# An encoder layer on one core: the MLP norm's scale moved into the first weights, its steps moved to ScalarE, a third tile for the mixers' output, query loads merged, and one combine of the differential attention moved to GpSimd

## The chip, the core and the metric

The kernel runs on one core of a Trainium2 chip. The metric is the time of one execution in device microseconds; for each kernel it is the median over several runs. TensorE is called PE in the profile (its weight loads PEld), VectorE DVE, ScalarE ACT, GpSimd POOL, and SyncE, which here only issues transfers, SP.

## The reference, cut to what matters

```python
n = rms_norm(h, g_mix);  z = n @ w_in                      # 1280 tokens (1024 + 256), width 1024
# mixer A: 4 heads, two softmax maps per head
sc = q @ k.T * scale - slope * |i - j|;  pr = softmax(sc)   # two maps, c = 0, 1
w  = pr[c=0] - lam * pr[c=1];  oa = rms_norm(w @ v, g_subln) * 0.8
# mixer B: 8 query heads on 2 key heads, rotary positions, plain softmax
h  = h + concat(oa, ob) @ w_out
n2 = rms_norm(h, g_mlp)                                     # n2 = h * rstd(h) * g_mlp
a  = relu(n2 @ w_ff1);  h = h + (a * a) @ w_ff2             # 1024 -> 4096 -> 1024
h  = h + sigmoid(rms_norm(h, g_ple) @ w_gate) * (p @ w_proj)
y  = rms_norm(h, g_final)
```

All is float32. `n2 @ w_ff1` is the same whether `g_mlp` (one number per input column) scales the columns of n2 or the rows of w_ff1.

## The kernel before, in words

A float32 product is made of three products of a shorter format: each operand is split into a high half (a rounded copy, usually by ACT) and a low half (the difference, by DVE or POOL), and high x high, high x low and low x high are summed in PSUM. So every matrix that TensorE reads costs ACT a copy and DVE or POOL a subtraction.

**Stages by time.** Input projections run to about 205 us, attention with the output projection woven in to about 730, the rest of the output projection, the MLP's norm and its transposes to about 824, the first MLP product to 1192, the second to 1586, gate and final norm to the end.

**Attention.** `plan_unit` (L509) plans units of 256 queries: for mixer A one unit per head and query block (two row blocks i = 0, 1 of 128 queries, two maps cc = 0, 1 each), for mixer B one per query head. Each step is put into a numbered round: scores (`qk`, L545) and, a round later, their row reduction on DVE (`mx`, L556; for A together with the distance term, L564, for B L568), the exponential on ACT (`ex`, L573 or L576), the combine (`cb`, L579), then transposes (L605), their halves on ACT (L611) and DVE (L616), and the product with the values (`av`, L629). A unit in the first 1024 tokens is "full": its rows are 1024 wide. In `cb` a mixer-A row block takes the reciprocals of both row sums (L583, DVE), scales the first map on POOL (L584), makes `-lam / sum` (L585, DVE) and adds the scaled second map to the first (L586, DVE). Row block 0 is combined two rounds before row block 1; the transposes read both. Steps after the attention product (L640 to L669) use POOL too (L660 to L663).

`load_q` (L471) fetches the 256 queries of a unit twice, into partitions 0 to 63 and 64 to 127, in four transfers of 128 KB: two copies by two maps.

**The weave.** The side work (`side_work`, L852: the remaining query and key projections, then two passes of the output projection) is a generator. The loop over rounds (L874) takes pieces from it in proportion to each round's cost; a piece of cost 0.0 ends the side work of that round. So `for _ in range(Y[k]): yield 0.0` lets a round go by without filler. What is left of the side work after the last round is done in the loop at L1066.

**Output projection** (`out_proj`, L801). The first pass takes four of the eight heads' outputs, the second the other four. For each of ten token tiles it loads the mixers' output `mt` (512 KB, L820) into W6 and W7 in turn, and makes two groups of twelve products (`pso`). Its weights come through `opw_dma` and `opw_split` (ACT L797, POOL L798). `Y = (2, 0, 0)` gives the empty turns: between the weight splits, before the remaining splits, and after the load of the first tile.

**MLP norm** (`mlp_norm`, L935). When a token tile is done in the second pass, its rows are stored (`hd`), squared and summed on ACT (L943), `rsqrt` (L130) makes the reciprocal root in six steps that change between DVE and ACT (L133, L134, L135, L137, L138, L139), and DVE multiplies the rows by it and by `g_mlp` in two halves of 512 columns (L948). `g_mlp` lies as a full tile in the last columns of two MLP operand tiles (`gbc`), filled by a broadcast from memory (L915 to L919). Then come transposes (L960), copies (`nb`, L968), sums and differences of 128 x 512 (L989) for a seven-product scheme (a 2 x 2 block product with seven instead of eight block products), and high and low halves (`n_split`, L1055, L1056; `nhi`, `nlo`).

**First MLP product.** `w_ff1` comes in 16 column blocks of 256. `w1_load` (L929) fetches one in two halves of 512 KB into W8, W9 and W10 in turn (`w1r`). `w1_ops` (L1010) makes the seven weight operands of a block: sums on POOL (L1026, L1027, L1032, L1036; on DVE for block 0), high halves on ACT (L1020), low halves on DVE or POOL (L1021). It runs one block ahead, one step after each product. The first block is started early: its loads are asked for at the start of the loop at L1066.

**What sets the order.** Within an engine's queue the order is fixed when the program is built. The builder places instructions by its own estimate of times, with the program's order as priority, so a queue's order is not always that of the lines: the first `w_ff1` load is issued at 467.44 us, in the middle of the attention, although its line stands after it. Tags such as W8 name a place in SBUF; a new tile in it waits until the former one has been read.

## Time and profile before

| | us |
|---|---|
| median of 3 runs | 1740.61 (1740.08 to 1741.46) |
| the profiled execution | 1741.92 |
| its span, first to last instruction | 1740.1 |

The page gives each engine's busy time and share of the span. Groups of instructions are named line, engine, operation, output<-inputs. A wait is written as "who <- whom: total us, times, longest". In a timeline row the first number is the start, the second the length, both in us, and the bracket says how long the engine stood idle before it and what ended that. In a row of busy time by stretch come the stretch, its length, the busy time of each engine with its instructions, TensorE's granted clock, the share of time the 16 transfer engines were busy, and GB/s.

### The profile page before, as it was taken

How to read it: one execution, taken by the hardware profiler on the slowest of the kernel's cores; microseconds unless marked ns; L12 is line 12 of the kernel's file. 1: busy time of each engine (PE TensorE's matmuls, PEld its weight loads, DVE VectorE, ACT ScalarE, POOL GpSimd, SP SyncE). 2: the span in 40 equal slices, each digit the busy share in tenths (PEclk: the TensorE clock that was granted, in tenths of full speed). 3: DMA queues.
4: the chain of work that ended last, by engine and by line, in shares of the span. 5: the costliest groups of instructions: out<-in, count | busy, mean ns of one | idle time of the engine just before them, and what ended most of it. 6: DMA issues, size and time to landing. Idle time of an engine off the chain costs nothing.

```text
span 1740.1 us, 27190 instructions
## 1 busy us (share of the span) xinstructions
PE 1675.2 (96%) x9868; PEld 1494.0 (86%) x9868; DVE 1182.7 (68%) x2115; ACT 852.7 (49%) x1715; POOL 598.3 (34%) x549
## 2 busy tenths in 40 slices
PE   8999988999989999998999999999999999999997
PEld 8999877888878887878999999998888888888886
DVE  7857468778778887579866666665664855354665
ACT  7522267767767666456333333333333333344554
POOL 1324445645654444431523332320433400001442
PEclk9999999999999999999999999999999999999999
DMA  9723653432873532282534333339665365532111
GB/s 306 229 80 109 194 163 104 121 122 86 235 207 105 157 103 79 92 271 87 182 130 152 128 131 141 142 137 385 232 227 194 120 209 191 179 112 83 39 44 49
DMA packets 188598, 263.45 MB, mean 151 GB/s; under 512 B 13104, under 2 KB 121520, under 8 KB 188464
## 3 DMA queue, kind: packets, MB, share of 16 engines
q1 hardware_dynamic: 186864, 256.47, 45.7%
q0 software_dynamic: 1600, 5.24, 1.0%
q8 instruction: 78, 1.28, 0.3%
q14 instruction: 56, 0.46, 0.1%
HBM read 175.16 MB, written 81.27 MB: 147 GB/s over the span
## 4 chain that ended last, share of the span: by engine, by line
PE 80%; DVE 7%; DMA 6%; ACT 3%; issue 2%; POOL 1%; SPq 1%; POOLq 0%; DVEq 0%; ACTq 0%
PE psg L151 6%; PE pso L220 5%; PE sc L551 5%; PE av L629 5%; PE psa L220 5%; PE tr L605 3%; PE psb L220 3%; PE psv L220 2%; PE psp L151 1%; DVE p L564 1%; DVE p L586 1%; DMA xr<-in_xT 1%; DMA mt<-md 1%; DMA xt<-in_x 1%; DVE pl L616 1%
## 5 line engine op out<-in xcount | busy, mean ns | idle before, releaser
L551 PE MATMUL sc<-kt,qt 128*128 128x512 f32 (+1 forms) x576 | 156.5, 395 | 18.2 <-DVE mm L564 7.2
L1231 ACT ACTIVATE ao<-ar 128x1280 fp32r<-128x1280 f32 x56 | 71.2, 1272 | 190.9 <-PE f__16190 L151 37.8
L1233 DVE TENSOR_TENSOR ao<-ar,ao 128x1280 fp32r<-128x1280 f32 x56 | 94.4, 1686 | 100.8 <-ACT ao L1231 100.8
L616 DVE TENSOR_TENSOR pl<-tr,ph 128x512 fp32r<-128x512 f32 x204 | 137.8, 683 | 33.7 <-ACT ph L611 32.9
L611 ACT ACTIVATE ph<-tr 128x512 fp32r<-128x512 f32 x204 | 120.2, 596 | 76.6 <-PE tr L605 63.1
L551 PEld LDWEIGHTS sc<-kt,qt 128*128 128x128 f32 x576 | 100.0, 190 | 39.1 <-DVE mm L564 11.3
L220 PE MATMUL pso<-ow,mt 128*128 128x512 f32 x480 | 122.7, 402 | 5.9 <-ACT ow L797 3.3
L605 PE MATMUL tr<-ident,p 128*128 128x128 f32 x768 | 117.0, 276 | 10.0 <-DVE pl L616 9.5
L151 PE MATMUL psg<-gw,n 128*128 128x512 f32 (+1 forms) x504 | 114.9, 384 | 0.0
L605 PEld LDWEIGHTS tr<-ident,p 128*128 128x128 f32 x768 | 92.1, 142 | 26.5 <-issue 8.5
L220 PEld LDWEIGHTS pso<-ow,mt 128*128 128x128 f32 x480 | 89.7, 193 | 24.2 <-ACT ow L797 3.8
L151 PEld LDWEIGHTS psg<-gw,n 128*128 128x128 f32 x504 | 90.9, 188 | 19.0
L629 PE MATMUL av<-ph,vt 128*128 128x256 f32 x544 | 103.5, 292 | 0.1
L1020 ACT ACTIVATE w<-w1s 128x512 fp32r<-128x512 f32 x64 | 40.1, 627 | 122.4 <-POOL w1s L1036 6.5
L568 DVE TENSOR_REDUCE mm<-sc 128x1 f32<-128x1024 f32 (+1 forms) x80 | 83.7, 1054 | 15.1 <-PE sc L551 14.5
L590 POOL TENSOR_SCALAR p<-p,rl 128x1024 f32<-128x1024 f32 x64 | 76.0, 1189 | 47.7 <-DVE rl L588 40.5
L629 PE MATMUL av<-pl,vt 128*128 128x256 f32 x408 | 91.7, 307 | 0.0
L629 PEld LDWEIGHTS av<-ph,vt 128*128 128x128 f32 x544 | 84.1, 194 | 4.9 <-DVE h_sb L840 0.3
L564 DVE CUSTOM_DVE_ANT_0 p<-sc,dist 128x1024 f32<-128x1024 f32 x64 | 77.1, 1217 | 13.4 <-PE sc L551 6.6
L576 ACT ACTIVATE p<-sc,mm 128x1024 f32<-128x1024 f32 x64 | 71.4, 1116 | 24.9 <-DVE mm L568 17.2
L573 ACT ACTIVATE p<-p,mm 128x1024 f32<-128x1024 f32 x64 | 73.4, 1148 | 12.7 <-DVE mm L564 11.6
L1406 POOL TENSOR_TENSOR p_l<-pr,p_h 128x256 fp32r<-128x256 f32 x10 | 7.8, 782 | 182.7 <-ACT p_h L1405 182.7
(1510 smaller groups left out, 4713.0 us busy)
## 6 DMA issues: line engine op xcount, KB each, us to landing
ar<-ad SPq DMA_DIRECT2D x56, 640.0 KB, 4.1
w2r<-in_w_ff SPq DMA_DIRECT2D x56, 512.0 KB, 4.5
qt<-qd SPq DMA_DIRECT2D x160, 128.0 KB, 3.2
ad<-q SPq DMA_DIRECT2D x64, 320.0 KB, 2.2
w1r<-in_w_ff SPq DMA_DIRECT2D x32, 512.0 KB, 3.8
ad<-qs SPq DMA_DIRECT2D x48, 320.0 KB, 2.2
md<-ml SPq DMA_DIRECT2D x40, 256.0 KB, 2.6
mt<-md SPq DMA_DIRECT2D x20, 512.0 KB, 4.6
```

The lines of the kernel that those rows point to most:

```text
L151: PE.matmul(ps, a, b, start=start and i == 0, stop=stop and i == n - 1)
L220: PE.matmul(ps, a, b, start=i == 0, stop=i == n - 1)
L551: PE.matmul(ps[:, h0:h0 + n], shared["q"][:, cc, v, i * P:(i + 1) * P], kt[:, s0 + h0:s0 + h0 + n], start=v == 0, stop=v == 1)
L564: V.tensor_tensor_reduce(out=p[:, :sn], in0=ps[:, :sn], in1=dst_t[:, off:off + sn], scale=SLOPES[idx], scalar=3.0e38, op0=ALU.add, op1=ALU ...
L568: V.tensor_reduce(out=st["m", i][:, 0:1], in_=ps[:, :sn], axis=AX.X, op=ALU.max, negate=True)
L573: S.activation(p[:, :sn], p[:, :sn], AF.Exp, scale=-1.0, bias=st["m", i][:, cc:cc + 1], accum_out=st["l", i][:, cc:cc + 1])
L590: G.tensor_scalar(p[:, :sn], p[:, :sn], rl[:, 0:1], 1.0, op0=ALU.mult, op1=ALU.mult)
L605: PE.transpose(t[:, jj, i * P:(i + 1) * P], st["ws"][i][:, j * P:(j + 1) * P], ident)
L611: S.activation(ph, st["tr", j2], AF.Copy)
L616: V.tensor_tensor(pl, st["tr", j2], f(st["ph", j2][:]), op=ALU.subtract)
L629: PE.matmul(st["av"][:, :256], x_, y_, start=j2 == 0 and n == 0, stop=j2 == nj - 1 and n == len(pr) - 1)
L1233: V.tensor_tensor(ao[:, 1], a, f(ao[:, 0]), op=ALU.subtract)
```

## The change

It does seven things.

1. `g_mlp` is loaded as a column tile (4 KB, after `gple`), the broadcast copy `gbc` and its loads are gone, and `w1_ops` first multiplies each of a block's eight weight slices (128 x 256) by its column of `g_mlp`, in place, on POOL.
2. `mlp_norm` runs on ACT alone: after the square, seven instructions on 128 x 1 (logarithm, mean plus eps, exponential, and one refinement step in four), then one copy of 128 x 1024 scaled by the result. DVE's two multiplications are gone.
3. `mt` gets W8 as a third place, in the whole first pass and in the first six tiles of the second; the last four tiles alternate between two.
4. As W8 is taken until then, the loads of the first block of `w_ff1` are asked for when six tiles of the second pass are done.
5. `Y = (2, 0, 2)`: two empty turns after the load of the first tile, in each pass.
6. `load_q` uses two transfers of 256 KB; the layout of `qt` is (operand half, map) in one index.
7. In `cb`, row block 0 of a full mixer-A unit scales the second map on POOL (by `-lam / sum`, in place) and adds the two maps on POOL. Row block 1 and the units of 256 tokens stay as they were.

```diff
-    Y = (2,0,0)
-    QM = 0
+    Y = (2,0,2)
...
+    gmlp = cp.tile([P, KD], F32, name="gmlp")
+    eps6 = cp.tile([P, 1], F32, name="eps6")
+    V.memset(eps6, 1e-6)
+    c15 = cp.tile([P, 1], F32, name="c15")
+    V.memset(c15, 1.5)
...
     gple = col("gple", g_ple, KD)
+    load(gmlp, g_mlp)
...
-        "qt": ([P, 2, 2, 256], F32R, QTB), "p": ([P, 1024], F32, PB), "dist": ([P, DISTW], F16, 1),
+        "qt": ([P, 4, 256], F32R, QTB), "p": ([P, 1024], F32, PB), "dist": ([P, DISTW], F16, 1),
...
         for dup in range(2):
-            for c in range(2):
-                dma(f(qt[dup * 64:(dup + 1) * 64, c]),
-                    qd[i][:, c * 64:(c + 1) * 64, t0:t0 + 256].rearrange("v d t -> d v t"))
+            dma(f(qt[dup * 64:(dup + 1) * 64]),
+                qd[i][:, :, t0:t0 + 256].rearrange("v (c d) t -> d (v c) t", d=64))
...
-                    PE.matmul(ps[:, h0:h0 + n], shared["q"][:, cc, v, i * P:(i + 1) * P],
+                    PE.matmul(ps[:, h0:h0 + n], shared["q"][:, 2 * v + cc, i * P:(i + 1) * P],
...
                 G.tensor_scalar(p[:, :sn], p[:, :sn], rl[:, 0:1], 1.0, op0=ALU.mult, op1=ALU.mult)
-                V.tensor_scalar(rl[:, 1:2], rl[:, 1:2], neglam, None, op0=ALU.mult)
-                V.scalar_tensor_tensor(p[:, :sn], p1[:, :sn], rl[:, 1:2], p[:, :sn], op0=ALU.mult, op1=ALU.add)
+                if i == 0 and full:
+                    G.tensor_scalar(p1, p1, rl[:, 1:2], neglam, op0=ALU.mult, op1=ALU.mult)
+                    G.tensor_tensor(p, p, p1, op=ALU.add)
+                else:
+                    V.tensor_scalar(rl[:, 1:2], rl[:, 1:2], neglam, None, op0=ALU.mult)
+                    V.scalar_tensor_tensor(p[:, :sn], p1[:, :sn], rl[:, 1:2], p[:, :sn], op0=ALU.mult, op1=ALU.add)
...
-            mt = slot(f"W{6 + next(mt_n) % 2}", [P, 4, 2, P], F32R, "mt")
+            mt = slot(("W6", "W7", "W8")[it % 3 if first or it < 6 else it % 2], [P, 4, 2, P], F32R, "mt")
...
-    gbc = [f(LO[i][:, :, HT - P:]) for i in (2, 3)]
-    gd = dp.tile([1, D], F32, name="gd")
-    dma(gd, g_mlp)
-    for i in range(2):
-        dma(gbc[i], gd[:, i * 512:i * 512 + 512].to_broadcast([P, 512]).rearrange("p (k t) -> p k t", t=P))
...
         S.activation(hn[t], h, AF.Square, accum_out=ss)
-        rs = ntp.tile([P, 1], F32, tag="nrs", name="nrs", bufs=2)
-        rsqrt(rs, ss, 1.0 / D, 1e-6, ntp, 1, f"n{half}")
-        for i in range(2):
-            c = slice(i * 512, i * 512 + 512)
-            V.scalar_tensor_tensor(hn[t][:, c].rearrange("p (k t) -> p k t", t=P),
-                                   h[:, c].rearrange("p (k t) -> p k t", t=P), rs, gbc[i], op0=ALU.mult, op1=ALU.mult)
+        u, v, rs = (ntp.tile([P, 1], F32, tag=f"n{n}{half}", name=f"n{n}", bufs=1) for n in "uvr")
+        S.activation(u, ss, AF.Ln, scale=1.0 / D, bias=eps6)
+        S.activation(v, ss, AF.Identity, scale=1.0 / D, bias=eps6)
+        S.activation(rs, u, AF.Exp, scale=-0.5)
+        S.activation(u, rs, AF.Square)
+        S.activation(u, u, AF.Copy, scale=v)
+        S.activation(u, u, AF.Identity, scale=-0.5, bias=c15)
+        S.activation(rs, rs, AF.Copy, scale=u)
+        S.activation(hn[t], h, AF.Copy, scale=rs)
...
         r0, r1 = w1raw.pop(p)
+        for k in range(KD):
+            r = (r0, r1)[k // 4][:, k % 4]
+            G.tensor_scalar(r, r, gmlp[:, k:k + 1], 1.0, op0=ALU.mult, op1=ALU.mult)
...
-        if n == 0:
+        if len(op_done) >= 6 and ops0 is None:
             w1_load(0, 0)
             w1_load(0, 1)
             ops0 = w1_ops(0)
```

More of the change, by code (lines that the diff above doesn't have):

```diff
@@ L473, in load_q @@
         for dup in range(2):
-            if QM:
-                dma(f(qt[dup * 64:(dup + 1) * 64]), qd[i][:, :, t0:t0 + 256].rearrange("v (c d) t -> d c v t", d=64))
-                continue
-            for c in range(2):
-                dma(f(qt[dup * 64:(dup + 1) * 64, c]),
-                    qd[i][:, c * 64:(c + 1) * 64, t0:t0 + 256].rearrange("v d t -> d v t"))
+            dma(f(qt[dup * 64:(dup + 1) * 64]),
+                qd[i][:, :, t0:t0 + 256].rearrange("v (c d) t -> d (v c) t", d=64))
         return qt
@@ L777, in encoder_kernel @@
     ow_n = itertools.count()
-    mt_n = itertools.count()
     def opw_dma(ch):
@@ L1056, in n_split @@
         lo_eng.tensor_tensor(LO[i][:, :, c], src, f(HI[i][:, :, c]), op=ALU.subtract)
-    trs, steps, normed = transposes(), 0, 0
+    trs, steps, normed, ops0 = transposes(), 0, 0, None
     w1raw = {}
@@ L1504 @@
         "w_gate": c(np.asarray(w_ple_gate)[0]), "w_proj": c(np.asarray(w_ple_proj)[0]),
-        "g_mix": c(np.asarray(g_mix)[0].reshape(KD, P).T), "g_mlp": c(np.asarray(g_mlp)[0].reshape(1, D)),
+        "g_mix": c(np.asarray(g_mix)[0].reshape(KD, P).T), "g_mlp": c(np.asarray(g_mlp)[0].reshape(KD, P).T),
         "g_ple": c(np.asarray(g_ple)[0].reshape(KD, P).T), "g_subln": c(np.asarray(g_subln)[0].reshape(P, 1)),
```

## The prediction

> **What bounds the kernel now.** I read the page's engine totals first, then busy time by stage, then the list of what TensorE waited for.
>
> ```profile
> PE 1675.2 (96%) x9868; PEld 1494.0 (86%) x9868; DVE 1182.7 (68%) x2115; ACT 852.7 (49%) x1715; POOL 598.3 (34%) x549
> ```
> ```profile
> 205.00:730.00 525.00, 488.76 (x3010) 425.15 (x3010) 404.93 (x741) 352.51 (x718) 262.68 (x275) 0.98 0.47 135
> 770.00:782.00 12.00, 11.49 (x60) 9.58 (x59) 11.31 (x22) 7.10 (x17) 4.40 (x6) 1.00 1.04 313
> 782.00:800.00 18.00, 17.25 (x97) 15.89 (x97) 17.58 (x30) 13.81 (x28) 2.29 (x4) 1.00 0.41 138
> 800.00:824.00 24.00, 18.96 (x127) 17.90 (x126) 23.65 (x39) 14.46 (x25) 3.53 (x3) 0.86 0.21 67
> 824.00:1192.00 368.00, 368.00 (x2505) 368.00 (x2504) 243.26 (x410) 130.60 (x258) 125.40 (x89) 1.00 0.43 153
> ```
> ```profile
> PE tr L605 <- DVE pl L616: 9.5, 13, 1.8
> PE sc L551 <- DVE mm L564: 7.2, 9, 2.0
> PE sc L551 <- ACT p L576: 6.0, 6, 1.7
> PE sc L551 <- DMA qt<-qd: 4.6, 1, 4.6
> PE pso L220 <- ACT ow L797: 3.3, 2, 3.1
> PE pso L220 <- DMA mt<-md: 2.6, 2, 2.1
> PE f__10380 L151 <- ACT nhi L1055: 2.1, 1, 2.1
> ```
>
> After the stretch come its length and the busy time of PE, PEld, DVE, ACT and POOL. TensorE is busy 96% of the span and never stops in the first MLP stage (368.00 of 368), so only its waits can be won, and nearly all of them lie in the attention (205 to 730 us) and in the passage to the MLP (730 to 824 us). In the attention they end mostly on DVE or on ACT work that DVE released. From 770 to 824 us DVE is the full engine: 52.5 of 54 us, beside ACT's 35.4.
>
> **The combine of the first map sum, attention.** One unit, in order of time:
>
> ```profile
> 637.89 1.12 POOL L584 TENSOR_SCALAR p<-p,rl 128x1024 f32<-128x1024 f32 x1 [6.17 <-PE sc L551]
> 639.05 1.28 DVE L586 SCALAR_TENSOR_TENSOR p<-p,rl 128x1024 f32<-128x1024 f32 x1 [0.38 <-POOL p L584]
> 640.25 1.22 DVE L564 CUSTOM_DVE_ANT_0 p<-sc,dist 128x1024 f32<-128x1024 f32 x1
> 641.53 1.19 PE L551 MATMUL sc<-kt,qt 128*128 128x512 f32 x4 [2.02 <-DVE mm L564]
> ```
> ```profile
> 239.60 0.44 PE L605 MATMUL tr<-ident,p 128*128 128x128 f32 x2 [1.17 <-DVE pl L616]
> 711.52 0.30 PE L605 MATMUL tr<-ident,p 128*128 128x128 f32 x1 [1.78 <-DVE pl L616]
> ```
> ```profile
> L586 DVE SCALAR_TENSOR_TENSOR p<-p,rl x32: 1264/1359/2235, 235.1 to 714.9; 128x1024 f32<-128x1024 f32 x32
> L1239 POOL TENSOR_TENSOR kt<-w2r,kt x8: 2392/2407/3320, 1295.5 to 1344.1; 128x1024 f32<-128x1024 f32 x8
> ```
> ```profile
> 297.49:304.15 6.66, 5.00 (x7) 1.00 0.67 192
> 422.86:429.77 6.91, 5.42 (x6) 1.00 0.48 141
> sum 149.76, POOL 74.63; mean POOL 4.66
> ```
>
> The first combine (row block i = 0) even makes DVE wait for POOL (0.38 us), and the next score reduction, for which TensorE waits, stands behind it. I followed every such wait back through DVE's unbroken busy run: 20 of them, the first at 239.60 and the last at 711.52 us, 17.9 us together, have a first combine in that run. They belong to 13 of the 16 full mixer-A units. Capped at what the edit takes out of the run (a combine of about 1.4 us and a 128x1 scale of about 0.2, like the small DVE step L138 quoted with the norm below), they are 15.9 us: the most that can be won.
>
> DVE loses 16 x (1.36 + 0.21) = 25 us of 404.93. POOL gets per unit a scale like L584 (1.12 us) and an add; the nearest row for that is L1239's median, 2.41 us. That is 3.53 us a unit, 56 us in all: POOL goes to 319 of 525 us. It must fit between a unit's two POOL scales, for the second combine stays on DVE behind the second scale. The 16 intervals last 149.76 us and POOL is busy for 74.63 of them, so 4.7 us are free on average; the two tightest, quoted, leave 1.66 and 1.49, one more 3.25. There the second scale comes 1.9, 2.0 and 0.3 us late, 4.2 us in all. The transposes need both row blocks, and the second is combined 7 to 14 us after the first, so the first one's longer POOL path holds nobody. Ends -15.9 (every wait goes) and +4.2 (none goes, every lateness is paid). I take -7, somewhat under half, because the exponentials and copies on ACT come next: at 711.52 TensorE waited for a low half that also needs ACT's high half.
>
> The Trainium skill, "SBUF — State Buffer", section "Who interferes with whom", says that a DVE instruction with two SBUF inputs and a GpSimd one that reads SBUF shut each other out for the whole instruction. The trace agrees: L586 takes 1264 ns alone and up to 2235. By that rule a 2.41 us add can hold a second combine for its whole length, at most 16 x 2.41 = 39 us of DVE time, where the rows of L586 give the -7 above.
>
> **Two more empty turns before the first output tile.**
>
> ```profile
> 700.00:720.00 20.00, 17.22 (x103) 14.65 (x103) 16.71 (x29) 13.85 (x29) 12.28 (x14) 0.91 0.04 14
> ```
>
> In the first pass this moves the first tile two rounds back, behind the weight split that TensorE awaited for 3.1 us (L797). The loop has some 220 rounds, 525/220 = 2.4 us each. In the quoted stretch they ran without filler and TensorE idled 14%, 0.33 us a round. So -3.1 + 0.7 = -2.4; ends -3.1 and +1.4 (the wait stays and the idle share doubles). The second pass has no such wait: +0.7, ends 0 and +1.4. The filler itself is only done later.
>
> **Third tile for the mixers' output, and the first MLP weights after it.**
>
> ```profile
> 745.14 7.79 DMA mt<-md
> 752.98 6.12 PE L220 MATMUL pso<-ow,mt 128*128 128x512 f32 x19 [2.12 <-DMA mt<-md]
> ```
>
> In the second pass the sixth tile was loaded when the fourth was done, took 7.79 us and cost 2.1. With three places it is asked for a tile earlier: -2.1. The last four tiles have two places again, so the other 0.5 us of this wait stays. The place is W8, so the first two w_ff1 loads (1 MB) now come when the sixth tile, begun at 752.98, is done, not long before the transfers are full (share 1.04 at 313 GB/s from 770 us): 3.4 us of transfer ahead of the eighth to tenth tiles. TensorE has transposes there; I take +0.7. Sum -1.4, ends -2.6 and +1.3 (all 3.4 against the 2.1). On SP these loads wait for W8; behind them stand tile loads whose place is free only two tiles later. In the first pass the third place frees SP from waiting, but no wait of TensorE there ends on mt: 0.
>
> **The norm on ACT.** The last tile's path now:
>
> ```profile
> 793.65 1.05 ACT L943 ACTIVATE hn<-h_sb 128x1024 f32<-128x1024 f32 x1
> 797.76 0.15 DVE L133 TENSOR_SCALAR n1v<-nss 128x1 f32<-128x1 f32 x1
> 798.42 0.19 ACT L134 ACTIVATE n1u<-n1v 128x1 f32<-128x1 f32 x1
> 800.95 0.21 DVE L138 SCALAR_TENSOR_TENSOR n1v<-nrs,n1v 128x1 f32<-128x1 f32 x1
> 802.96 1.41 DVE L948 SCALAR_TENSOR_TENSOR hn<-h_sb,nrs,nlo 128x512 f32<-128x512 f32 x2
> 803.85 1.79 PE L960 MATMUL trn<-ident,hn 128*128 128x128 f32 x8 [2.77 <-ACT nhi L1055]
> ```
>
> From the square's start to the transposes go 10.2 us, most of it in DVE's queue. As a row on ACT: 1.05 + 7 x 0.2 + 1.05 = 3.5 us. A tile takes 1.9 us off DVE (0.15, 0.21, one more such small step, 1.41) and puts 1.8 on ACT (four more small steps, one copy of 128x1024 like the square). With four tiles normalised from 770 to 824 us, DVE goes from 52.5 to 45, ACT from 35.4 to 43 of 54 us. But from 782 to 800 us ACT gets 13.81 + 2 x 1.8 = 17.4 of 18 and becomes the full engine. The waits to be had are 2.8 and 2.1, 4.9 us. I take -2, ends -4.9 and +2 (one tile's extra ACT work in front of the high halves).
>
> **The scale folded into w_ff1, on POOL.**
>
> ```profile
> L584 POOL TENSOR_SCALAR pq<-pq,rl x8: 477/482/1559, 293.4 to 674.2; 128x256 f32<-128x256 f32 x8
> 820.19 0.63 ACT L1020 ACTIVATE w<-w1r 128x512 fp32r<-128x512 f32 x1 [4.76 <-DMA w1r<-in_w_ff]
> 820.31 1.29 POOL L1026 TENSOR_TENSOR w1s<-w1r 128x512 f32<-128x512 f32 x1 [25.52 <-DMA w1r<-in_w_ff]
> 821.68 1.62 POOL L1027 TENSOR_TENSOR w1s<-w1r,w1s 128x512 f32<-128x512 f32 x1
> 823.91 1.55 PE L151 MATMUL f__10596<-nhi,w 128*128 128x384 f32 x8
> 781.30 1.22 PE L151 MATMUL f__10336<-nhi,w 128*128 128x384 f32 x6
> ```
>
> Eight scales of 128x256 at 0.48 us are 3.84 us a column block. The first block's, on weights that land some 10 us after the sixth tile, are done well before its first product, now at 781.30: 0, and 3.84 without that cover. From the third block on it is covered: each weight is split a whole unit, 7 x 3.5 = 24.5 us, before its product, and POOL goes to 125.40 + 15 x 3.84 = 183 of 368 us. Without that cover it would cost 58 us. The second block has little cover: landing at 820.2, scales to 824.0, the two differences to 826.9, split on ACT and DVE (0.63 + 0.69) to 828.2, while the second product is due at 823.91 + 3.5 = 827.4. So +0.8; ends 0 (the half that landed early is scaled first) and +3.8.
>
> **The rest.**
>
> ```profile
> 220.00:225.00 5.00, 0.75 (x2) 0.69 (x3) 0.90 (x2) 1.98 (x4) 1.95 (x2) 0.88 1.10 273
> ```
>
> Two query loads for four halve SP's issues, but the one wait for them (4.6 us) lies where the transfers are full (1.10) and the bytes are the same: 0, ends -4.6 (it goes) and +0.5 (TensorE now waits for a whole load, 128 KB more at 273 GB/s). The dropped broadcast of g_mlp and the added 4 KB load have no waiter: 0.
>
> **Sum** against the profiled execution, 1741.92 us (span 1740.1 and 1.8 around it): -7 - 2.4 + 0.7 - 1.4 - 2 + 0.8 = -11.3, so 1730.6. The median of the runs, 1740.61, lies 1.3 below the profiled one: 1729.3.
>
> **Rivals.**
> - *The attention's waits only move.* TensorE then waits for ACT, or for queues that the build's own ordering has laid out anew. For it: ACT is busy 67% there and releases the 6.0 us row. Against: in the unit at 637 us nothing but DVE stands between. Gain of the other terms alone: 1741.92 - 4.3 - 1.3 = 1736.3.
> - *POOL becomes the late engine, slower.* If the add takes 5 us, held off by DVE, the extra is 6.1 us a unit, and the 16 intervals are short by 27.6 us together. The second combine then heads DVE's queue and waits. With half of that on TensorE and the 7 us not won: 1730.6 + 7 + 13.8 - 1.3 = 1750. It decides once the add is over 3.6 us (4.7 free less 1.12). Against it: L1239's slowest is 3320 ns. The skill's SBUF page, by the rule above, is what would make it so.
> - *All waits behind the first combine and in the passage go.* -15.9 and -4.9 in place of -7 and -2: 1729.3 - 8.9 - 2.9 = 1717.5.
>
> **Chances.** Forecast 0.60 (its own range 1722 to 1738), waits move 0.20, POOL late 0.10, all go 0.10. A measurement of this kernel can tell about 0.2%, 3.5 us. The first rival lies near that bound, some of it inside; with the forecast's upper edge that makes faster 0.79, same 0.11, slower 0.10. The range, 1716 to 1743, leaves out the slower rival and the outermost of the rest.
>
> **What would show it.** Right: between 205 and 730 us DVE near 380 us and POOL near 320; the three DVE-bound rows of TensorE's waits down by about 7 us; the row on L797 gone; mt waits under 1.5; the last tile's square to transposes under 6 us; TensorE still 100% busy in the first MLP stage, with at most 2 us lost before its second block. Wrong: a POOL add over 3.6 us or DVE idle behind POOL at the second combine; ACT full from 782 to 800 us with high halves later; a new wait on mt after 765 us; an attention stretch of 525 us or more.

## The result, and the profile after

The changed kernel is slower: 1755.72 us (median of four runs, 1752.23 to 1757.44) against 1740.34 (median of four, 1739.75 to 1741.46). The ratio is 1.0085, 95% interval 1.0067 to 1.0103. The profiled execution of the changed kernel took 1752.23 us, with a span of 1750.5; it is the fastest of its four, so the two profiles show 10.3 of the 15.4 us between the medians.

The page first, with the engine totals, and then busy time by stage (stretch, length, PE, PEld, DVE, ACT, POOL, PE's granted clock, transfer share, GB/s):

```profile
PE 1682.0 (96%) x9868; PEld 1494.7 (85%) x9868; DVE 1158.5 (66%) x2035; ACT 870.4 (50%) x1765; POOL 717.9 (41%) x709
```
```profile
205.00:730.00 525.00, 484.89 (x2980) 416.62 (x2979) 381.22 (x707) 351.48 (x717) 310.78 (x307) 0.99 0.48 133
770.00:782.00 12.00, 12.00 (x62) 10.14 (x61) 7.50 (x13) 10.39 (x25) 5.97 (x9) 1.00 0.95 304
782.00:800.00 18.00, 17.60 (x96) 15.48 (x95) 15.50 (x20) 15.96 (x33) 3.74 (x5) 1.00 0.71 221
800.00:824.00 24.00, 14.53 (x77) 13.39 (x76) 19.21 (x27) 19.93 (x38) 8.53 (x9) 0.72 0.08 26
824.00:1192.00 368.00, 367.46 (x2498) 367.19 (x2497) 253.55 (x408) 127.82 (x256) 187.66 (x202) 1.00 0.42 143
```

The loads moved between engines as forecast: in the attention DVE went from 404.93 to 381.22 and POOL from 262.68 to 310.78. But TensorE was busy for less there (484.89 instead of 488.76), and from 800 to 824 us it fell from 18.96 to 14.53, at a granted clock of 0.72 instead of 0.86. What TensorE waited for:

```profile
PE sc L552 <- ACT p L577: 14.3, 11, 6.7
PE tr L610 <- DVE pl L621: 10.2, 16, 1.7
PE trn L962 <- ACT hn L951: 9.4, 2, 6.4
...
PE sc L552 <- DVE mm L565: 5.4, 7, 1.2
...
PE pso L224 <- ACT ow L801: 1.0, 1, 1.0
...
PE f__10577 L155 <- DVE w L1026: 0.5, 1, 0.5
```

The waits on `mt` (2.6 us before) and on the query loads `qt` (4.6) are gone, and that on `ow` is down from 3.3 to 1.0 us. The attention's waits on DVE have stayed: those on the reductions `mm` fell from 7.2 to 5.4, those on the low halves `pl` rose from 9.5 to 10.2. The waits on ACT's exponentials rose from 6.0 to 14.3, and there is a new row: the norm's transposes wait 9.4 us for ACT's copy `hn`.

Of the 14.3 us, 6.7 are one wait at the very start of the attention, and it goes with the query loads, not with the combine. TensorE waits there for an exponential, the exponential for row maxima on DVE, and these stand in DVE's queue behind a step on `zl`, which waited 7.49 us until a store (`kd<-zl`) had read its place:

```profile
220.18 0.69 DVE L742 SCALAR_TENSOR_TENSOR zl<-psa,R 128x512 f32<-128x512 f32 x1 [7.49 <-DMA kd<-zl]
222.03 1.11 ACT L577 ACTIVATE p<-sc,mm 128x1024 f32<-128x1024 f32 x1 [0.50 <-DVE mm L569]
223.29 3.78 PE L552 MATMUL sc<-kt,qt 128*128 128x512 f32 x8 [6.73 <-ACT p L577]
```

All thirteen kernels of this case that merge the query loads have this wait (5.3 to 6.8 us) and none on `qt`. The seven that do not have 3.3 to 4.6 us on `qt` at the same place.

**A table by stage** serves all that follows. Its marks are TensorE's own products in the trace: the first score product, the last product of the output projection, the end of the first column block of the first MLP product (its 168th product), the start of the third block, the ends of the first and second MLP product and of the gate. All in us, from the profiled executions:

| kernel | attention and output projection | passage (of it to the last transposes) | second block | blocks 3 to 16 | second product | gate | from the third block on |
|---|---|---|---|---|---|---|---|
| before | 575.4 | 35.2 (16.8) | 24.5 | 345.8 | 390.2 | 142.9 | 878.8 |
| after | 574.5 | 42.6 (26.4) | 25.4 | 347.7 | 390.5 | 143.4 | 881.6 |

What comes before the first score product took 213.4 and 214.5 us, what follows the gate 12.7 and 11.8. So the 10.3 us of the profiles are 7.4 in the passage, 0.9 in the second block, 2.8 after it, and -1.0 in the attention's column, where -10.1 was forecast.

The 7.4 us of the passage have two parts. Its rows, before and after:

```profile
788.90:824.10 35.20, 29.41 (x188) 28.00 (x188) 34.85 (x56) 21.72 (x39) 4.38 (x4) 0.90 0.21 68
```
```profile
789.00:831.60 42.60, 32.73 (x197) 30.59 (x197) 36.01 (x53) 33.44 (x66) 14.71 (x18) 0.84 0.25 78
```

TensorE stands idle for 9.9 us in place of 5.8, and its granted clock is 0.840 on average in place of 0.903. As an estimate, that clock loses 42.6 x 0.160 = 6.8 us after and 35.2 x 0.097 = 3.4 before. So some 4 us are waits and the other 3.4 the lower clock.

### The profile page after: what moved, and what is told of

It is laid out like the page before. It is cut to its first block, busy times and chain, and to the rows that moved or that the text cites. A ratio compares the mean times of both kernels' runs of the same rounds, so it can differ in the third digit from the quotient of the medians.

```text
span 1750.5 us, 27208 instructions
## 1 busy us (share of the span) xinstructions
PE 1682.0 (96%) x9868; PEld 1494.7 (85%) x9868; DVE 1158.5 (66%) x2035; ACT 870.4 (50%) x1765; POOL 717.9 (41%) x709
## 4 chain that ended last, share of the span: by engine, by line
PE 81%; DVE 5%; DMA 5%; ACT 4%; issue 3%; POOL 2%; SPq 0%; DVEq 0%; ACTq 0%; POOLq 0%
PE psg L155 6%; PE sc L552 5%; PE pso L224 5%; PE psa L224 5%; PE av L634 4%; PE psb L224 4%; PE tr L610 3%; PE psv L224 3%; PE psp L155 2%; DMA h_sb<-in_w_out 1%; DVE pl L621 1%; ACT p L574 1%; DMA vt<-vbd 1%; DVE mm L569 1%; DVE p L565 1%
## 5 line engine op out<-in xcount | busy, mean ns | idle before, releaser
L552 PE MATMUL sc<-kt,qt 128*128 128x512 f32 (+1 forms) x576 | 158.1, 397 | 20.9 <-ACT p L577 14.3
L610 PE MATMUL tr<-ident,p 128*128 128x128 f32 x768 | 115.8, 274 | 12.6 <-DVE pl L621 10.2
L224 PE MATMUL pso<-ow,mt 128*128 128x512 f32 x480 | 117.2, 394 | 1.2 <-ACT ow L801 1.0
L1017 POOL TENSOR_SCALAR w1r<-w1r,gmlp 128x256 f32<-128x256 f32 x128 | 79.8, 641 | 89.7 <-DMA w1r<-in_w_ff 81.6
```

Source lines behind the costliest of these rows:

```text
L224: PE.matmul(ps, a, b, start=i == 0, stop=i == n - 1)
L552: PE.matmul(ps[:, h0:h0 + n], shared["q"][:, 2 * v + cc, i * P:(i + 1) * P], kt[:, s0 + h0:s0 + h0 + n], start=v == 0, stop=v == 1)
L610: PE.transpose(t[:, jj, i * P:(i + 1) * P], st["ws"][i][:, j * P:(j + 1) * P], ident)
L1017: G.tensor_scalar(r, r, gmlp[:, k:k + 1], 1.0, op0=ALU.mult, op1=ALU.mult)
```

## The experiments

Two things limit what the table can tell. The stretch ahead of the first score product, mostly loads, took 213.4 to 218.2 us in executions with the same instructions; it is left out. And five kernels with the same order of every engine's queue (the kernel before, and it with 32 to 128 unused bytes) had 571.4 to 575.4 us in the attention's column, mean 572.6; six that share TensorE's order with the changed kernel up to the last product with the values (changed, with 32 bytes, norm undone, copy on ACT, scale left out, sum aside) had 573.6 to 580.0, mean 576.0. So kernels with the same order differ by 4 to 6 us in that column, and a smaller difference between two single kernels is not read in it. From the third block on the times repeat to 0.1 us.

### One part undone at a time

**Norm undone** (back to the old steps and one multiplication on DVE):

```diff
-        S.activation(u, ss, AF.Ln, scale=1.0 / D, bias=eps6)
...
-        S.activation(hn[t], h, AF.Copy, scale=rs)
+        rsqrt(rs, ss, 1.0 / D, 1e-6, ntp, 1, f"n{half}")
+        V.tensor_scalar(hn[t], h, rs, None, op0=ALU.mult)
```

> The changed kernel with the norm's row taken back off ScalarE: the reciprocal root in its old six steps between VectorE and ScalarE, then one multiplication of 128 x 1024 by it on VectorE (the scale g_mlp stays in the first weights). Theory 1 (the row of seven small steps and the copy stand in ScalarE's full queue between 782 and 813 us, and the last transposes come 9.7 us later for it): 7 to 8 us less than the changed kernel, about 1.004 of the kernel before; the last transposes begin near 806 us instead of 813. Theory 2 (the loss sits in the scale of w_ff1 on GpSimd and the later loads of w_ff1): within 2 us of the changed kernel, 1.008 of the kernel before. Theory 3 (the attention's new queues lose it): also 1.008.

Measured: 1752.7 us, 1.0068 [1.0055, 1.0081]; passage 38.4 (18.3).

**Combine undone** (row block 0 on DVE as before):

```diff
-                if i == 0 and full:
-                    G.tensor_scalar(p1, p1, rl[:, 1:2], neglam, op0=ALU.mult, op1=ALU.mult)
-                    G.tensor_tensor(p, p, p1, op=ALU.add)
-                else:
-                    V.tensor_scalar(rl[:, 1:2], ...)
+                V.tensor_scalar(rl[:, 1:2], ...)
```

> The changed kernel with the combine of row block 0 back on VectorE, all else as changed. Theory 1 (the loss is the norm on ScalarE, and the combine on GpSimd only moved attention's waits to ScalarE): within 3 us of the changed kernel, 1.007 to 1.010 of the kernel before, with TensorE's waits on the low halves of the transposed maps back near 9.5 us and those on the exponential down from 14 to about 6. Theory 3 (the combine on GpSimd itself costs, or the attention's queues do): 4 to 8 us less than the changed kernel. The prediction's own view (the combine gains 7): 7 us more, 1.0125.

Measured: 1749.09 us, 1.0044 [1.003, 1.0059]; attention 567.6, passage 42.5 (25.5). From 213 to 735 us TensorE waits 9.5 us for exponentials and 12.3 for low halves.

**Third tile, later weights and empty turns undone** (`mt` in two places, loads at `n == 0`, `Y = (2,0,0)`):

> The changed kernel with the mixers' output in two places again, the first loads of w_ff1 asked for at the start of the last loop, and the empty turns as before. Theory 1: the third tile and the empty turns were worth 2 to 4 us, so 2 to 4 us more than the changed kernel (1.010 to 1.011). Theory 2 (late w_ff1 loads delay the first MLP products): 2 to 5 us less than the changed kernel (1.005 to 1.007). Theory 3 (the empty turns shift the output projection's first pass by 12 us, and it is paid for): 4 us less or more.

Measured: 1751.15 us, 1.0054 [1.0041, 1.0067]; attention 573.6, passage 43.9 (26.9), second block 24.7.

**Scale left out:**

```diff
-        for k in range(KD):
-            r = (r0, r1)[k // 4][:, k % 4]
-            G.tensor_scalar(r, r, gmlp[:, k:k + 1], 1.0, op0=ALU.mult, op1=ALU.mult)
```

> The changed kernel without the multiplication of w_ff1 by g_mlp on GpSimd: that scale is left out of the computation altogether, so this prices the 128 multiplications. Theory 1 (their price is hidden but for the second column block): 0 to 3 us less than the changed kernel, 1.007 to 1.0085 of the kernel before. Theory 2 (they stand ahead of the sums of the first blocks and hold the passage and the first MLP stage): 5 us or more less, 1.005 or lower, with the wait for the second block's weights (0.5 us) gone and the first MLP stage 3 us shorter.

Measured: 1755.1 us, 1.0076 [1.0063, 1.0089]; passage 41.9, second block 24.6, and still 881.6 from the third block on.

What follows: theory 1 (the norm alone) falls. It is right in its place, 4.2 us of the passage come back (3.0 by the ratio, where 7 to 8 were expected), but undoing the combine brings more, 6.9 us in the attention and 7 by the ratio, so theory 3 holds as well. Without the scale the second block is 0.8 us shorter and the passage 0.7, so theory 2 falls. What undoing the third tile did isn't settled: the ratio says some 5 us less than the changed kernel, its profile 0.7 more. And none of the four brings back the 2.8 us after the second block: a column block takes 24.83 us in all of them, 24.69 in the kernel before, with no wait in it.

### The place of the tiles

The changed kernel's three new constants take 96 bytes per partition, and the tiles behind them move by 96; the right-hand tiles, filled from the other end, stay. ("Left-hand" and "right-hand" mean the two ends of SBUF here, not the two sides of a product.) In the built programs the first of the MLP's operands on the left (`nlo`) begins at byte 17,760 before and 17,856 after, the first on the right (`nhi`) at 120,800 in both. Five kernels change only this, with

```diff
+    pad = cp.tile([P, 24], F32, name="pad_c")
+    V.memset(pad, 0.0)
```

(8, 16, 24, 32 numbers in the kernel before, 8 in the changed one). In each the order of the queues is that of the kernel it was made from, but for the one memset.

> The kernel before with 96 unused bytes per partition among its constants, as many as the change adds with its three new constants, so that the left-hand tiles lie 96 bytes further on, as they do in the changed kernel. Theory 4 (a part of the loss is only this shift: in all four kernels of the first call, and in the changed one, a column block of the first MLP product takes 24.83 us in place of 24.69, with no wait in it, even without the scale of w_ff1): 24.83 a block, so 2 us in this stage, and 2 to 4 us in all, 1.001 to 1.0025. Theory 2 (those 0.14 us come from the scale's or the split's new code): 24.69 a block and 1.000.

> The changed kernel with 32 more unused bytes per partition, so that the left-hand tiles lie 128 bytes from where they lie in the kernel before. Theory 4: 24.69 us a column block again and 2 to 4 us less than the changed kernel, 1.006 to 1.007 of the kernel before. Theory 2: 24.83 a block, 1.0085.

> The kernel before with 128 unused bytes per partition among its constants in place of 96: the left-hand tiles lie where they lie in the changed kernel with 32 bytes more. Theory 4 (the place of TensorE's operands in SBUF sets how fast its products run, whatever the change does): the second MLP product takes 383 us in place of 390, a column block of the first 24.59 in place of 24.69, gate and end 2 less, so some 10 us less, 0.994 of the kernel before. If what the change computes is needed for it: 1.000.

> The kernel before with 64 unused bytes per partition among its constants. Known: from the third block of the first MLP product to the end of the gate, 0 bytes give 345.8 + 390.2 + 142.9 us, 96 bytes 347.7 + 390.5 + 143.4, 128 bytes 344.5 + 382.9 + 140.7. If 128 is special (left-hand and right-hand tiles then lie alike within 256 bytes): 64 gives 345 to 348 and 390, 0.999 to 1.002 of the kernel before. If 0 and 96 are the bad places: 383, 0.995.

> The kernel before with 32 unused bytes per partition among its constants. From the third block of the first MLP product to the end of the gate: 0 bytes 345.8 + 390.2 + 142.9 us, 64 bytes 343.2 + 390.3 + 143.3, 96 bytes 347.7 + 390.5 + 143.4, 128 bytes 344.5 + 382.9 + 140.7. If only 128 is good for the second product: 390 here, and 0.999 to 1.002 in all. If 32 and 128 are alike: 383 and 0.995.

| unused bytes | ratio to the kernel before | blocks 3 to 16 | second product | gate | sum |
|---|---|---|---|---|---|
| 0 | 1 | 345.8 | 390.2 | 142.9 | 878.8 |
| 32 | 1.0028 [1.0018, 1.0039] | 345.8 | 391.4 | 144.1 | 881.2 |
| 64 | 0.9994 [0.9983, 1.0006] | 343.2 | 390.3 | 143.3 | 876.8 |
| 96 | 1.0012 [1.0003, 1.0022] | 347.7 | 390.5 | 143.4 | 881.6 |
| 128 | 0.9952 [0.9933, 0.997] | 344.5 | 382.9 | 140.7 | 868.1 |
| changed kernel, 32 more | 1.0011 [0.9998, 1.0023] | 344.5 | 382.9 | 140.7 | 868.1 |

Busy time by stage in the second product shows it without any mark: TensorE busy for all of 300 us at full clock, with a different number of products done (stretch, length, PE with its instructions, clock, transfer share, GB/s). The kernel before:

```profile
1250.00:1550.00 300.00, 300.00 (x1299) 1.00 0.55 180
```

The changed kernel, and it with 32 bytes more:

```profile
1250.00:1550.00 300.00, 300.00 (x1298) 1.00 0.57 183
```
```profile
1250.00:1550.00 300.00, 300.00 (x1324) 1.00 0.57 185
```

The kernel before with 128 bytes:

```profile
1250.00:1550.00 300.00, 300.00 (x1324) 1.00 0.55 180
```

A page that says "busy 100%" can hide 2%. Theory 4 holds: the shift by 96 bytes is the 2.8 us, and 32 bytes more take 13.5 us off the changed kernel without a change of order. The 343.2 at 64 bytes and the ratio at 32 lie outside what was expected of them, and the changed kernel with 32 more came out some 9 us below the 1.006 expected of it. Why 128 bytes suit the second product and 64 the first isn't shown. With 128, left-hand and right-hand tiles begin at the same remainder modulo 256 (17,888 and 120,800 both leave 224), which fits the second product, but the first is best at 64.

### The combine

**Combine alone**, in the kernel before (the diff of "combine undone", reversed):

> The kernel before with the combine of row block 0 on GpSimd and nothing else. Theory 3 (this part costs some 7 us by itself, whatever the rest): 5 to 8 us more, 1.003 to 1.005, the extra in the attention before its last product. The prediction (it gains 7): 0.996. Theory 1 (it only moves waits): within 2 us of 1.000.

Measured: 1746.58 us, 1.0026 [1.0015, 1.0037]; attention 576.0, passage 39.0 (16.9). TensorE's waits in the attention, which for the kernel before were 6.0 on `p`, 9.5 on `pl` and 7.2 on `mm`:

```profile
PE sc L551 <- ACT p L576: 10.5, 13, 1.6
PE tr L609 <- DVE pl L620: 9.9, 15, 1.7
...
PE sc L551 <- DVE mm L564: 3.2, 4, 1.2
```

Four us leave the rows that end on DVE's reductions and 4.5 come back on those that end on ACT's exponentials. By the ratio this kernel loses 4.5 us, less than theory 3 expected and more than theory 1. In its profile the attention is 3.4 us above the mean of 572.6, within the spread, and the passage 3 to 4 us above the 34.9 to 35.9 of its five kin, though nothing in it was changed. Three kernels then take the added work apart.

**Nothing in its place** (neither POOL step):

```diff
-                    G.tensor_scalar(p1, p1, rl[:, 1:2], neglam, op0=ALU.mult, op1=ALU.mult)
-                    G.tensor_tensor(p, p, p1, op=ALU.add)
+                    pass
```

> The changed kernel without the two GpSimd steps of row block 0 (the second map is not scaled and not added there, on any engine: that part of the computation is left out), so VectorE keeps its relief and GpSimd gets no more work. Theory 3a (VectorE's relief is worth something, and GpSimd's longer path to the transposes and to the freed map buffers takes it away and more): 8 us or more below the changed kernel, and below the one with the combine back on VectorE: 1.000 to 1.003. Theory 3b (VectorE's relief is worth nothing, since ScalarE comes next): as with the combine on VectorE, 1.004. Theory 3c (the new order of the queues, not GpSimd's work, costs it): still 1.007 or more.

Measured: 1733.13 us, 0.9944 [0.9929, 0.9959]; attention 552.4.

**Sum aside** (same work, but the transposes don't need the sum):

```diff
-                    G.tensor_tensor(p, p, p1, op=ALU.add)
+                    G.tensor_tensor(p1, p, p1, op=ALU.add)
```

> The changed kernel with the sum of row block 0 written over the second map, which nothing reads then (the second map's part of row block 0 is left out of the computation): GpSimd does the same work and holds the same buffers, but the transposes do not wait for its last two steps. From the first score to the last product of the output projection the changed kernel takes 574 us, the one without the two steps 552. Theory 3a (the transposes wait for the longer path): 552 to 557, 0.995. Theory 3d (GpSimd's queue, with the steps that stand behind the two, or the second map's buffer that comes free later): 570 to 575, 1.007 or more.

Measured: 1755.34 us, 1.0078 [1.006, 1.0097]; attention 575.2.

**Second map free at once** (same work on the first map):

```diff
-                    G.tensor_scalar(p1, p1, rl[:, 1:2], neglam, ...)
-                    G.tensor_tensor(p, p, p1, op=ALU.add)
+                    G.tensor_scalar(p, p, rl[:, 1:2], neglam, ...)
+                    G.tensor_tensor(p, p, p, op=ALU.add)
```

> The changed kernel with both added GpSimd steps of row block 0 made on the first map alone (the second map is left out of the computation there): the same work on GpSimd and the same path to the transposes, but the second map's buffer is free at once, as in the kernel without the two steps. Theory 3e (the buffer that comes free later holds the next distance step on VectorE): 552 to 560 us for the stage, 0.995 to 0.999. Theories 3a and 3d (path or queue): 570 to 575, 1.007 or more.

Measured: 1752.09 us, 1.0055 [1.0037, 1.0074]; attention 569.1. Busy time from 213 to 735 us of the one with nothing in its place, and of this one:

```profile
213.00:735.00 522.00, 496.54 (x3070) 432.76 (x3069) 381.76 (x715) 361.96 (x752) 257.06 (x282) 0.99 0.49 140
```
```profile
213.00:735.00 522.00, 487.55 (x2997) 421.81 (x2996) 377.21 (x709) 352.50 (x719) 300.71 (x305) 0.98 0.47 133
```

Leaving the first combine out altogether is worth much, 15 us against the combine on DVE (567.6 to 552.4). The work on POOL costs 17 of it back (552.4 to 569.1), more than the 552 to 560 us of theory 3e allow. With the second map's buffer held as well it is 6 more (575.2), at the edge of what the column tells; the intervals of the two ratios overlap. TensorE's idle time in the column (36.1, 25.3, 34.3 and 38.6 us in these four) holds 11, 9 and 4 us of the three steps. The rest is time that counts as busy, in part at a lower granted clock (0.991, 0.991, 0.982 and 0.985). The path to the transposes, theory 3a, costs nothing: "sum aside" has the changed kernel's queues instruction for instruction, and its time. Whether POOL's time does it or the order that the builder then lays out is open: TensorE's order differs in some hundred places between "nothing in its place" and "second map free at once", as between the latter and the changed kernel, and no run here holds the order while it changes GpSimd's time.

### What is left when the parts are put together

**Copy on ACT** (old steps, last multiplication on ACT):

```diff
+        rsqrt(rs, ss, 1.0 / D, 1e-6, ntp, 1, f"n{half}")
         S.activation(hn[t], h, AF.Copy, scale=rs)
```

> The changed kernel with the root in its old six steps between VectorE and ScalarE, and the copy of 128 x 1024 scaled by it still on ScalarE. From the last output product to the last transpose the changed kernel takes 26 us, the one with the old steps and the multiplication on VectorE 18. If the row of seven small steps in ScalarE's queue is what delays them: 17 to 20 us, and 3 to 4 us less than the changed kernel, 1.0065 of the kernel before. If the copy on the full ScalarE is: 24 to 27 us, 1.008.

Measured: 1753.77 us, 1.0068 [1.0052, 1.0083]; passage 40.3 (17.7). So the row of small steps is what delays the last transposes, by 8.6 us; but the copy on ACT gives some of that back, since the first MLP products then wait for ACT:

```profile
PE f__10300 L155 <- ACT nb L963: 2.8, 1, 2.8
...
PE f__10395 L155 <- ACT q L1137: 2.2, 1, 2.2
```

**Combine and norm undone, with 32 bytes:**

> The changed kernel with the combine back on VectorE, the norm back in its old steps, and 32 unused bytes: what is left of the change is the third tile, the later first weights, the empty turns, the merged query loads and the scale of w_ff1 on GpSimd. If the terms add up: attention with output projection 567 to 569 us, passage 38, the later stages as with the 128 bytes above, so 1724 to 1728 us, 0.991 to 0.993 of the kernel before. If the attention's gain without the combine (7 us) was an accident of the queues' order: 1731 to 1734, 0.995.

Measured: 1736.38 us, 0.9965 [0.9951, 0.9978]; attention 570.7, passage 36.8 (17.0), second block 26.1.

**Third tile, empty turns, query loads alone, with 128 bytes:**

> The kernel before with three parts of the change alone (third tile with the later first weights, the empty turns, the merged query loads) and 128 unused bytes per partition. If the attention's gain without the combine holds: attention with output projection 567 to 571 us against 572 of the kernel before with the 128 bytes, passage 35 to 37, the second block of w_ff1 without its wait (1.7 less than with the scale on GpSimd), so 1724 to 1729 us and 0.990 to 0.993 of the kernel before. If it was an accident of the queues' order: as with the 128 bytes alone, 0.995 to 0.996.

Measured: 1738.41 us, 0.9979 [0.9966, 0.9992]; attention 571.7, passage 43.2 (21.6). The attention gains nothing against the 128 bytes alone (572.0), and the passage is 7.3 us longer than with those alone (35.9): TensorE is idle for 8.5 us in place of 6.5, and its granted clock there is 0.80 in place of 0.90. With the same three parts and the scale, "combine and norm undone" had 36.8 us at 0.91.

**The same with half the combine on POOL:**

```diff
+                if i == 0 and full:
+                    G.tensor_scalar(p1[:, 512:], p1[:, 512:], rl[:, 1:2], 1.0, op0=ALU.mult, op1=ALU.mult)
+                    G.tensor_tensor(p[:, 512:], p[:, 512:], p1[:, 512:], op=ALU.add)
+                n = 512 if i == 0 and full else sn
```

> The last kernel with row block 0's combine split by columns: the first 512 stay on VectorE, GpSimd scales and adds the other 512 (some 1.8 us a unit on GpSimd in place of 3.6; nothing is left out). If GpSimd's added time costs what VectorE's relief brings: within 3 us of the last kernel. If its cost is in proportion (17 us for the whole against a relief of 15): 0 to 2 us more. If only the whole is too long for the gap between a unit's two scales: 4 to 8 us less.

Measured: 1734.88 us, 0.9959 [0.9943, 0.9974]; attention 568.3, passage 41.8. That is 3.5 us less than the last kernel, between what was expected, and its 3.4 us in the attention are within the spread.

**Half the combine alone, with 128 bytes:**

> The kernel before with 128 unused bytes and the first combine split by columns (512 on VectorE, 512 scaled and added on GpSimd); nothing else of the change. If half the combine on GpSimd is a gain by itself: attention with output projection 567 to 569 us against 572 with the 128 bytes alone, and 0.992 to 0.994 of the kernel before. If it moves waits only, as the whole did in the kernel before (576 against 575): 571 to 574 and 0.995.

Measured: 1734.38 us, 0.9964 [0.9951, 0.9978]; attention 572.1, passage 36.2. Against the 128 bytes alone (572.0) nothing.

The terms do not add up: "combine and norm undone" and the next one came out 8 to 14 us above the first figures expected of them. The passage takes 35 to 36 us in the kernel before wherever its tiles lie, 41.9 to 43.9 with the norm on ACT, but also 43.2 with the old norm and the later weights, and 36.8 when the scale is on POOL as well. No one part decides it, and where it is long the granted clock is low as well. That the order of the queues does it is likely, but no run holds that order and changes the rest. The lowest ratio of all kernels that leave nothing out is that of the kernel before with 128 unused bytes: 1733.95 us, 0.9952. Nothing of the change, laid on top of it, was measurably faster.

## Why the prediction was wrong

It forecast 1729.3 and gave slower a chance of 0.10; 1755.72 lies outside its range. Its sum was -11.3 and the two profiles show +10.3. Of these 21.6 us, 9.1 lie in the attention's column, 9.4 in the passage (+7.4, where the norm's -2 was to fall) and 2.8 behind the second block. By its own steps:

**The combine, "I take -7": this step failed.** Against 567.6 to 571.7 us in three kernels without the combine on POOL and with the other parts (mean 570.0), the changed one and its kin have 573.6 to 580.0 (mean 576.0). So it cost about 6 us in place of the gain of 7; undone it is 7 us by the ratio, alone 4.5. TensorE's idle time rose by 2.6 of the 6 (36.8 to 39.4 us on average), so the waits that were to go only changed their ends. Durations were right: 2393 ns for the add, forecast 2.41 us (name, engine, shapes, count, busy us and mean ns, idle before).

```profile
L588 POOL TENSOR_TENSOR p<-p 128x1024 f32<-128x1024 f32 x16 | 38.3, 2393 | 0.4
L585 POOL TENSOR_SCALAR p<-p,rl 128x1024 f32<-128x1024 f32 x32 | 36.0, 1124 | 34.2 <-DVE rl L584 32.2 <-PE tr L610 1.4 <-PE av L653 0.2
...
L587 POOL TENSOR_SCALAR p<-p,rl,neglam 128x1024 f32<-128x1024 f32 x16 | 19.1, 1195 | 0.0
```

What failed is the counting of cost at one place, the gap between a unit's two scales (4.2 us late in all), and of gain at another, waits with a combine in DVE's run. The 57 us of POOL work cost 17 in the stage although by that count the gaps hold all but 4.2 of it, and leaving the combine out is worth 15, more than 7. Right was that the longer path of the first row block holds nobody ("sum aside"). The bound on DVE's loss that the prediction worked out from the rule of the Trainium skill's "SBUF — State Buffer" page ("Who interferes with whom"), 39 us, is far from the trace. A combine on DVE takes 1615 ns on average in the changed kernel, 1489 with the combine undone, so the 16 that are left lose 16 x 0.126 = 2 us. The changed kernel, then the other:

```profile
L591 DVE SCALAR_TENSOR_TENSOR p<-p,rl 128x1024 f32<-128x1024 f32 x16 | 25.8, 1615 | 0.7 <-POOL p L585 0.6
```
```profile
L587 DVE SCALAR_TENSOR_TENSOR p<-p,rl 128x1024 f32<-128x1024 f32 x32 | 47.6, 1489 | 2.7 <-POOL p L585 2.6
```

The first rival named the mechanism, waits that move to ACT, and "combine alone" shows it row by row; its price, 1736.3, left out what the move costs. The second, POOL late because of a slow add, is excluded by the 2393 ns. The third's bound of -15.9 came true only where POOL got no work.

**The norm, "I take -2": this step failed.** It rested on "as a row on ACT: 1.05 + 7 x 0.2 + 1.05 = 3.5 us". The last tile's steps on ACT, in order of time:

```profile
803.11 1.06 ACT L941 ACTIVATE hn<-h_sb 128x1024 f32<-128x1024 f32 x1
...
805.71 0.28 ACT L943 ACTIVATE nu<-nss,eps 128x1 f32<-128x1 f32 x1
805.89 0.28 ACT L944 ACTIVATE nv<-nss,eps 128x1 f32<-128x1 f32 x1
806.08 0.62 ACT L1060 ACTIVATE nhi<-nt 128x512 fp32r<-128x512 f32 x1
806.60 0.62 ACT L1060 ACTIVATE nhi<-h_sb 128x512 fp32r<-128x512 f32 x1
807.12 0.20 ACT L945 ACTIVATE nr<-nu 128x1 f32<-128x1 f32 x1
807.21 1.06 ACT L970 ACTIVATE nb<-trn 128x512 f32<-128x512 f32 x2
808.16 0.20 ACT L947 ACTIVATE nu<-nr 128x1 f32<-128x1 f32 x1
...
811.19 0.30 ACT L948 ACTIVATE nu<-nu,nv 128x1 f32<-128x1 f32 x1
811.52 0.29 ACT L949 ACTIVATE nu<-nu,c 128x1 f32<-128x1 f32 x1
811.85 0.29 ACT L950 ACTIVATE nr<-nr,nu 128x1 f32<-128x1 f32 x1
812.18 1.15 ACT L951 ACTIVATE hn<-h_sb,nr 128x1024 f32<-128x1024 f32 x1
```
```profile
805.34 1.66 PE L962 MATMUL trn<-ident,hn 128*128 128x128 f32 x8 [2.99 <-ACT hn L951]
813.38 1.97 PE L962 MATMUL trn<-ident,hn 128*128 128x128 f32 x8 [6.38 <-ACT hn L951]
```

The steps do not run in a row. The high halves and copies stand between them in ACT's queue, and square to transposes takes 10.3 us, as long as the 10.2 before, beginning 9.5 us later: the square itself waits its turn on an engine (ACT is the fourth number after the length) that is busy for 27.19 of 28 us:

```profile
785.00:813.00 28.00, 18.51 (x100) 15.85 (x98) 23.30 (x29) 27.19 (x56) 11.79 (x14) 0.87 0.41 133
```

With the norm undone, the transposes of the last two tiles wait much less:

```profile
805.88 1.07 PE L955 MATMUL trn<-ident,hn 128*128 128x128 f32 x8 [1.78 <-ACT nhi L1053]
808.42 1.94 PE L955 MATMUL trn<-ident,hn 128*128 128x128 f32 x8 [1.47 <-ACT nb L963]
```

The prediction's warning, "ACT becomes the full engine", was the sign to follow. So the norm on ACT costs 4.2 us here, and 5.7 between "combine undone" (42.5) and it with the norm undone as well (36.8, with 32 bytes), in place of the gain of 2. Of the 4.2, 3.3 are TensorE's idle time (9.9 to 6.6 us) and the rest goes with its granted clock (0.840 to 0.867). The other 3.2 of the 7.4 are not pinned to a part.

**Two terms that the sum lacked.** One is the granted clock: the sum counts waits alone, but in the passage the clock fell from 0.903 to 0.840 when they grew. The other is where the tiles lie. "The added 4 KB load has no waiter: 0" counted the new constants as free. They moved every left-hand tile by 96 bytes, +2.8 us.

**Right in their waits, not in their time.** The empty turns and the third tile: the wait on `mt` went and that on `ow` fell by 2.3 us. With the combine on DVE the attention has 570.0 against 572.6, -2.6 where -2.4 + 0.7 - 1.4 = -3.1 was said, but a difference of this size is within what the column leaves open, and with the combine on POOL nothing of it is seen (573.6 undone). The later first weights, taken as +0.7, are not safe at that price: put on the kernel before with 128 bytes, these parts made the passage 7.3 us longer.

**Right.** The scale: the second block loses 0.8 us (25.4 against 24.6 with the scale left out), as forecast, though over the kernels with the scale it takes 24.7 to 26.1. POOL is busy for 187.66 us of the first MLP stage, forecast 183, but that is luck in part: one slice takes 641 ns, not 480, and other rows on POOL fell (the difference on L1032 before, L1037 after, from 27.8 to 20.0 us in this stage).

```profile
L1017 POOL TENSOR_SCALAR w1r<-w1r,gmlp 128x256 f32<-128x256 f32 x128 | 79.8, 641 | 89.7 <-DMA w1r<-in_w_ff 81.6 <-DVE nlo L1061 5.7 <-issue 1.7
```

The query loads, taken as 0: the wait on `qt` went, but the wait behind `zl` at the same place came with it (6.3 us of waits in the first units before, 7.1 after). The 0 is right, by a path that the prediction did not see. The merged loads weren't tried alone.

What isn't explained: the 5.1 us of the medians' difference that the profiled execution, the fastest of four, doesn't hold.

## What to carry to other kernels

A chain of short dependent steps pays for each step the queue of the engine it is put on, not only its own 0.2 us; before it is gathered on one engine, look at what else that engine has in that stretch. Free time on an engine, even in the very gaps where the work fits, isn't the price of the work: take the work out on both sides (leave it out; do it with nobody waiting) before crediting the relief. Where waits grow, look at the granted clock beside them: it took nearly half of what the passage lost here. And a change that adds a constant moves tiles, so compare it with a kernel before that has the same bytes unused.

## What was not expected of the hardware

TensorE's speed depended on where the left-hand tiles begin in SBUF, tried in steps of 32 bytes: with the same instructions in the same order, busy 100% at a granted clock of 1.00, the second MLP product took 382.9 to 391.4 us and blocks 3 to 16 of the first 343.2 to 347.7. In the second product nearly all products begin 226 or 227 ns after the one before with 128 bytes, and 224 to 238 ns with none. Only the place of these tiles differs between those kernels; what in it costs the time is not shown. From the third block on the spread is 868.1 to 881.6 us, 13.5 us, nearly the 15.4 by which the medians of the two kernels differ.

A multiplication of 128 x 1024 by one column took DVE 0.75 us as a tensor-scalar instruction ("norm undone", L944: median 753 ns of ten, the slowest 917), half of the 1.41 that the kernel before needed with `g_mlp` as a second tile in two instructions of 512 (L948).
